# Prompt attention scores on two row halves of TensorE, sampled value products in one shape, sampled blocks in twos, seven cache buffers

## The chip, the cores and the metric

The kernel runs on one core of one Trainium2 chip. The metric is the device time of one execution in microseconds (us); lower is better. The core has TensorE (PE in the profile; its loads of the stationary operand are listed as PEld), VectorE (DVE), ScalarE (ACT), GpSimd (POOL) and SyncE (SP), whose queue issues most of the DMAs. TensorE multiplies a stationary operand, held in an array of 128 rows (contraction) by 128 columns (output partitions), by a moving operand that streams through it.

## The reference

One step of a streaming encoder with two layers: a convolution layer, then an attention layer, each followed by a SwiGLU feed-forward block. Two groups go through it together: 512 prompt frames of one new stream, and 16 frames of each of 8 running streams (the samples). Only the attention is touched. There are 16 heads of 64 features. The prompt attends to its own keys, in chunks of 64 frames, with a learned bias by distance; a sample attends to 512 cached keys and its own 16 new ones:

```
def band_attention_sample(q, k_all, v_all, table):
    s = jnp.einsum("bqhd,bkhd->bhqk", q, k_all) * scale + bias
    p = jax.nn.softmax(s, axis=-1)
    return jnp.einsum("bhqk,bkhd->bqhd", p, v_all)
# prompt, for each chunk of 64 queries: the same over the 576 keys that end with the chunk,
# keys ahead of the stream's start masked with -1e30
```

All is 32-bit floating point.

## The kernel before

All activations are kept with features on the partitions: `h` is 128 x 8 x 640, the first 128 of the 640 columns being the samples and the other 512 the prompt. Weight products that need full precision split both operands into a high part (`fp32r`, a rounded type of 32 bits) and the low rest and add three products, high x high, low x high, high x low (`mm3`, L196 to L202). The program runs the convolution layer, the first feed-forward block, the attention stage (about 694 to 1002 us of the profiled execution) and the second feed-forward block.

*The attention stage* works through 8 pairs of heads (the loop at L1418). For each pair `proj_kq` projects keys and queries of the pair into `kt` and `qt`, 128 x 640, where rows 0 to 63 are the first head and 64 to 127 the second. `proj_v` projects values for two pairs at once, `proj_o` and `halves` the output. The order of a pair's own steps is written out by hand in the strings `BO` (pairs 0 to 6) and `BL` (the last pair) at L67 and L68; each token is a letter for the step and a digit for its instance:

- `a` (`head_a`, L1259): the prompt scores of one head, its row maxima and its softmax. A head has 64 features, half of the array's rows, so the kernel fills the other half with low parts: `QQ` holds the query's high part in the head's own rows and its low part in the other rows; `KK` holds the key's high part in both halves, `KL` the key's low part in both. Then two matmuls per query tile on all 128 rows (L1285, L1286) give all products. The four query tiles need 512, 384, 128 and 256 key columns, in this order (`ORD`). Making `KK`, `KL` and `QQ` takes two ScalarE copies (L1271, L1272), one GpSimd copy (L1273) and three VectorE subtractions (L1275 twice, L1277), all on 64 rows x 512. Scores go to PSUM: three tiles to `wide`, the fourth to a part of `st`, both from the two large buffers of `w2t()`. `addmax` (L1193) adds the bias and takes the row maximum on VectorE, `softmax_rows` takes exponentials on ScalarE.
- `s` (`samp_a`, L1331): the scores of four streams, for both heads of the pair: loads four cache tiles, two of keys and two of values, from a pool of `CB = 8` buffers (L1337, on SP's queue); then matmuls with 32 stationary columns for each stream, so that four streams fill the four column strips of the array (form 128\*32; L1342 for cached keys, L1345 for new ones), into `st` of the head before; then bias, maximum, exponentials.
- `b` (`head_b`): transposes the prompt's probabilities; `t` and `n` (`samp_b` and its `rest`): transpose the sampled ones, `t` for the 512 cached keys, `n` for the 64 new ones (L1364).
- `p` (`pair_c`, L1318): the prompt's value product, each head on 64 of the array's columns (form 128\*64).
- `c` (`samp_c`, L1371): the sampled value product, four streams on four column strips, in five steps: four over cached values on 128 rows (L1378, form 128\*32) and one over the new values on the 64 rows of this block (L1382, form 64\*32).
- `d`: scales, transposes and splits the sampled output (L1386 to L1397).
- `o`, `q` in `BL`: one or two steps of an output projection (`halves`), placed there as filler.

Transposes, value products and the `d` steps share the two PSUM buffers of `amt()`; projections use the two of `mmt()`. The strings give the order of priority. Each engine's final order is fixed when the program is built: TensorE's queue takes matmuls of a projection where the next step of the pair would have to wait. `qt` has one buffer and `kt` two.

Of the kernel before, what the change touches and what calls it, by code (L numbers as in the profile page):

```python
# [15 lines left out]
P = 128  # L16
# [42 lines left out]
CB, QB, KB = 8, 1, 1  # L59
# [7 lines left out]
BO = "a0 s0 a1 s1 b0 b1 t0 n0 p0 c0 d0 t1 n1 c1 d1"  # L67
BL = "a0 o2 s0 a1 o2 s1 q2 t0 q2 n0 b0 q2 b1 q2 c0 q2 d0 t1 q2 n1 o2 c1 o2 d1 p0 o2"  # L68
# [14 lines left out]
def tile_trunk(ctx, tc, xT, vecs, hist, w_pw1, w_pw2, w_in0, w_out0, w_os0, w_in1, w_out1, w_os1,  # L83
# [1052 lines left out]
    nc.gpsimd.memset(BP[:, :, 0:256], 0.0)  # L1136
    BS = ap.tile([P, 576], F32, name="BS", tag="BS")
# [121 lines left out]
    def head_a(p, hh):  # L1259
        kt, qt = kts[p], qts[p]  # L1260
        r = slice(hh * DH, hh * DH + DH)
        S = sp.tile([P, 1280], F32, tag="S", name=nm("S"))
        mx = ap.tile([P, 4], F32, tag="mx", name=nm("mx"), bufs=3)
        sm = ap.tile([P, 4], F32, tag="sm", name=nm("sm"), bufs=3)
        wide = w2t()
        st = w2t()
        ro = slice(DH - hh * DH, 2 * DH - hh * DH)
        KK = ap.tile([P, 512], F32R, tag="KK", name=nm("KK"), bufs=KB)
        KL = ap.tile([P, 512], F32R, tag="KL", name=nm("KL"), bufs=KB)
        QQ = ap.tile([P, 512], F32R, tag="QQ", name=nm("QQ"), bufs=KB)  # L1270
        nc.scalar.activation(out=KK[r], in_=kt[r, P:], func=AF.Copy)  # L1271
        nc.scalar.activation(out=QQ[r], in_=qt[r, P:], func=AF.Copy)  # L1272
        nc.gpsimd.tensor_copy(KK[ro], KK[r].bitcast(F32))  # L1273
        for to in (r, ro):
            nc.vector.tensor_tensor(out=KL[to], in0=kt[r, P:], in1=KK[r].bitcast(F32),  # L1275
                                    op=ALU.subtract)
        nc.vector.tensor_tensor(out=QQ[ro], in0=qt[r, P:], in1=QQ[r].bitcast(F32),  # L1277
                                op=ALU.subtract)
        pss = []
        for i in ORD:  # L1280
            n = (i + 1) * P
            o = SOFF[i]
            q = slice(i * P, (i + 1) * P)
            ps = st[:, 640:896] if i == 1 else wide[:, o:o + n]
            nc.tensor.matmul(ps, QQ[:, q], KK[:, 0:n], start=True, stop=False)  # L1285
            step_end[0] = nc.tensor.matmul(ps, QQ[:, q], KL[:, 0:n], start=False, stop=True).ins  # L1286
            pss.append(ps)
        for ii, i in enumerate(ORD):
            n = (i + 1) * P
            o = SOFF[i]  # L1290
            addmax(S[:, o:o + n], pss[ii], BP[:, hh, 512 - n:512], mx[:, ii:ii + 1])
        rs = softmax_rows(S, mx, sm, [(SOFF[i], (i + 1) * P) for i in ORD])
        for ii, i in enumerate(ORD):
            n = (i + 1) * P
            o = SOFF[i]
            nc.vector.tensor_scalar(out=S[:, o:o + n], in0=S[:, o:o + n],
                                    scalar1=rs[:, ii:ii + 1], scalar2=None, op0=ALU.mult)
        return S, st
# [32 lines left out]
    def samp_a(p, u, st):  # L1331
# [18 lines left out]
        addmax(S, st[:, 0:576], BS, mx[:, 0:1])  # L1350
# [3 lines left out]
    def samp_b(u, S):  # L1354
        v0 = 64 * u
        tr = amt()
        for k in range(4):
            step_end[0] = nc.tensor.transpose(tr[:, k * P:(k + 1) * P],
                                              S[:, k * P:(k + 1) * P], ident).ins
        PT = ap.tile([P, 640], F32, tag="PTs", name=nm("PTs"), bufs=1)  # L1360

        def rest():
            tn = amt()
            step_end[0] = nc.tensor.transpose(tn[0:v0 + 64, 0:P], S[:, 512 - v0:576], ident).ins  # L1364
            nc.vector.tensor_copy(PT[v0:v0 + 64, 512:640], tn[v0:v0 + 64, 0:P])
            return PT

        nc.scalar.activation(out=PT[:, 0:512], in_=tr, func=AF.Copy)
        return rest

    def samp_c(p, u, PT, rs, VC):  # L1371
        v0 = 64 * u
        VT = vts[p // 2]
        pv = amt()
        for k in range(5):
            for b in range(4):
                if k < 4:
                    nc.tensor.matmul(pv[32 * b:32 * b + 32, 0:P],  # L1378
                                     PT[:, k * P + 32 * b:k * P + 32 * b + 32],
                                     VC[b // 2][:, b % 2, k * P:(k + 1) * P], start=(k == 0), stop=False)  # L1380
                else:
                    step_end[0] = nc.tensor.matmul(  # L1382
                        pv[32 * b:32 * b + 32, 0:P],
                        PT[v0:v0 + 64, 512 + 32 * b:512 + 32 * b + 32],
                        VT[v0:v0 + 64, 0, (p % 2) * P:(p % 2) * P + P], start=False, stop=True).ins
        os_ = ap.tile([P, P], F32, tag="os", name=nm("os"), bufs=1)  # L1386
# [31 lines left out]
    for p in range(NP):  # L1418
# [8 lines left out]
        for op in (BL if p == NP - 1 else BO).split():  # L1427
            i = int(op[1])
            if op[0] == "a":
                ha[i] = head_a(p, i)  # L1430
            elif op[0] == "s":
                sa[i] = samp_a(p, i, ha[i][1])
            elif op[0] == "b":
                pt[i] = head_b(ha[i][0])
# [4 lines left out]
            elif op[0] == "c":  # L1439
                ps[i] = samp_c(p, i, ps[i], *sa[i][1:])  # L1440
# [247 lines left out]
```

## Time and profile before

| | |
|---|---|
| three runs | 1458.16, 1460.51, 1463.31 us; median 1460.51 |
| span of the profiled execution | 1460.0 us, 28194 instructions |
| TensorE busy | 1434.0 us (98%) |
| VectorE, ScalarE, GpSimd busy | 1138.9, 757.8, 297.6 us |
| granted TensorE clock | 0.999 of full speed |
| DMA over the span | 192.56 MB, 132 GB/s |

The time of the profiled execution outside its span is not given; the span lies within the three runs. A row of a group names the line, the engine, the operation, output<-inputs, for TensorE the array's shape in use (rows\*columns), the moving operand, and a count; then the busy time in us, the mean of one in ns, and the idle time ahead of it with what ended it. A row of the timeline begins with start and length in us; instructions of one line that follow each other are merged into one row, with their count. Matmuls overlap in the array, so the step from one start to the next says more than the length. Operations on 4-byte data that are not `fp32r` run as two passes, each with a row of its own.

### The profile page before, as it was taken

The numbers are of one execution on the slowest core, as the hardware profiler recorded it, in microseconds if no ns is written. First come the engines' busy times: TensorE is split into PE (matmuls) and PEld (weight loads), VectorE is DVE, ScalarE is ACT, GpSimd is POOL, SyncE is SP. The second block draws the span as 40 slices with busy tenths as digits, with TensorE's granted clock in tenths as the row PEclk, the third lists the DMA queues.
The fourth block names the chain that finished last, engine by engine and source line by source line (L and its number), as shares of the span: only waits on it lengthen the run. The fifth ranks groups of instructions, "written<-read, shape, count | busy, mean of one in ns | idle before, by whom it ended". The sixth has DMA issues, their size and how long they took to land. (4 is left out here: it accounts for less than half of the span.)

```text
span 1460.0 us, 28194 instructions
## 1 busy us (share of the span) xinstructions
PE 1434.0 (98%) x11022; PEld 1369.6 (94%) x11022; DVE 1138.9 (78%) x2520; ACT 757.8 (52%) x1628; POOL 297.6 (20%) x349
## 2 busy tenths in 40 slices
PE   9999999999999999999999999999999999999998
PEld 8998799999999999999987898878999999999998
DVE  6789867988888888756768668577898888888765
ACT  4666554654554554545654355443554564455453
POOL 5699120010111111013222121011011111111101
PEclk9999999999999999999999999999999999999999
DMA  7267434045444534425556554452125444444522
GB/s 243 73 180 187 126 86 146 14 135 150 131 108 118 163 92 135 116 88 193 181 163 213 173 192 162 138 200 67 44 82 143 135 113 129 137 120 109 155 66 72
DMA packets 66932, 192.56 MB, mean 132 GB/s; under 512 B 12144, under 2 KB 30320, under 8 KB 58480
## 3 DMA queue, kind: packets, MB, share of 16 engines
q1 hardware_dynamic: 52432, 160.58, 33.8%
q0 software_dynamic: 13504, 29.37, 9.9%
q8 instruction: 86, 1.41, 0.4%
q10 hardware_dynamic: 864, 0.83, 0.2%
q14 instruction: 46, 0.38, 0.1%
HBM read 179.14 MB, written 11.61 MB: 131 GB/s over the span
## 5 line engine op out<-in xcount | busy, mean ns | idle before, releaser
L439 PE MATMUL mm<-XH,whi 128*128 128x320 f32 x896 | 275.9, 310 | 2.9 <-ACT t L451 2.6
L439 PE MATMUL mm<-XH,wlo 128*128 128x320 f32 x896 | 276.1, 309 | 0.0
L439 PE MATMUL mm<-XL,whi 128*128 128x320 f32 x896 | 274.5, 309 | 0.0
L371 ACT ACTIVATE whi<-raw 128x512 fp32r<-128x512 f32 (+2 forms) x280 | 168.4, 613 | 135.2 <-PE mm L439 103.6
L199 PE MATMUL mm<-xh,whi 128*128 128x320 f32 (+2 forms) x640 | 200.2, 314 | 0.8 <-DVE h L702 0.4
L200 PE MATMUL mm<-xh,wlo 128*128 128x320 f32 (+2 forms) x640 | 198.2, 311 | 0.0
L372 DVE TENSOR_TENSOR wlo<-raw,whi 128x512 fp32r<-128x512 f32 (+2 forms) x280 | 183.9, 666 | 15.9 <-ACT whi L371 14.8
L201 PE MATMUL mm<-xl,whi 128*128 128x320 f32 (+2 forms) x640 | 195.9, 311 | 0.4 <-DVE xl L189 0.4
L439 PE MATMUL mm<-hid,whi 128*128 128x320 f32 x732 | 172.5, 311 | 5.5 <-DVE hid L372 3.1
L439 PEld LDWEIGHTS mm<-XH,whi 128*128 128x128 f32 x896 | 167.7, 188 | 4.9 <-ACT t L451 4.2
L439 PEld LDWEIGHTS mm<-XH,wlo 128*128 128x128 f32 x896 | 168.2, 188 | 0.0
L439 PEld LDWEIGHTS mm<-XL,whi 128*128 128x128 f32 x896 | 167.7, 188 | 0.0
L439 PEld LDWEIGHTS mm<-hid,whi 128*128 128x128 f32 x732 | 125.0, 188 | 8.8 <-DVE hid L372 4.2
L199 PEld LDWEIGHTS mm<-xh,whi 128*128 128x128 f32 x640 | 120.5, 188 | 4.0 <-ACT xh L187 1.5
L201 PEld LDWEIGHTS mm<-xl,whi 128*128 128x128 f32 x640 | 119.7, 188 | 1.2 <-DVE xl L189 0.8
L200 PEld LDWEIGHTS mm<-xh,wlo 128*128 128x128 f32 x640 | 120.5, 189 | 0.2
L439 PE MATMUL mm<-hid,wlo 128*128 128x320 f32 x366 | 113.0, 309 | 0.0
L439 PE MATMUL mm<-XH,slo 128*128 128x320 f32 x344 | 106.0, 308 | 0.0
L439 PE MATMUL mm<-XH,shi 128*128 128x320 f32 x344 | 105.8, 309 | 0.0
L439 PE MATMUL mm<-XL,shi 128*128 128x320 f32 x344 | 105.6, 308 | 0.0
L417 POOL DMA_DIRECT2D s<-in_w_in x38 | 22.1, 581 | 388.7 <-DVE wlo L372 151.8
L841 POOL TENSOR_TENSOR ca<-ca,cvt 128x512 f32<-128x512 f32 x60 | 91.9, 1532 | 17.8 <-ACT cvt L838 11.2
(275 smaller groups left out, 3370.8 us busy)
## 6 DMA issues: line engine op xcount, KB each, us to landing
raw<-in_w_in SPq DMA_DIRECT2D x38, 1024.0 KB
s<-in_w_in POOLq DMA_DIRECT2D x76, 256.0 KB, 4.2
raw<-in_w_os SPq DMA_DIRECT2D x24, 768.0 KB
cache<-in_ck SPq DMA_DIRECT2D x32, 512.0 KB
cache<-in_cv SPq DMA_DIRECT2D x32, 512.0 KB
raw<-in_w_pw SPq DMA_DIRECT2D x11, 1024.0 KB
s<-in_w_os POOLq DMA_DIRECT2D x48, 192.0 KB, 3.6
raw<-in_w_kq SPq DMA_DIRECT2D x8, 1024.0 KB
```

Of the source, the lines that this page charges most:

```text
L199: nc.tensor.matmul(ps, wh, xh, start=(first and i == 0), stop=False)
L200: nc.tensor.matmul(ps, wl, xh, start=False, stop=False)
L201: end = nc.tensor.matmul(ps, wh, xl, start=False, stop=(stop and i == last))
L371: put_end[1] = nc.scalar.activation(out=hi, in_=src, func=AF.Copy).ins
L372: put_end[0] = nc.vector.tensor_tensor(out=lo, in0=src, in1=hi.bitcast(F32), op=sub).ins
L417: nc.gpsimd.dma_start(s1, src[:, 2 * n:3 * n])
L439: last = nc.tensor.matmul(pt, wt, v, start=(first and k == i == 0), stop=(k == n - 1 and i == 2), skip_group_check=True)
L841: nc.gpsimd.tensor_tensor(out=acc, in0=acc, in1=pr, op=ALU.add)
```

## The change

1. `head_a` gives up its score matmuls. A new `heads_split` makes the scores of both heads at once, when token `a0` is reached: the high and low parts are made for both heads together on 128 rows x 512 (two ScalarE copies, two VectorE subtractions a pair, no GpSimd copy), and each head's three products run on its own 64 rows, the two heads alternating. Three query tiles of each head go to a large buffer of its own; the fourth goes to a buffer of `amt()`.
2. `samp_a` takes its own large buffer (`w2t()`) in place of `st`.
3. The fifth step of `samp_c` uses 128 rows: the transposed probabilities of the new keys (`pn`) are padded with zeros in the rows of the other block, from `Sn` (zeros in columns 576 to 639) or in `PN` (zeros in rows 0 to 63), both set once. The scaled output `os_` now lies in the block's own probability tile.
4. `BO` and `BL` put `a0 a1`, `s0 s1`, `t0 n0 t1 n1` (in `BO`) and `c0 c1`, `d0 d1` together; in `BO` the pair product `p0` comes ahead of `c0`, as before, now with `c1` behind `c0`.
5. `CB` is 7: seven cache buffers for the eight cache tiles of a pair. `Ss` has one buffer (and `Sn`), `PTs` two.

```
-CB, QB, KB = 8, 1, 1
+CB, QB = 7, 1
-BO = "a0 s0 a1 s1 b0 b1 t0 n0 p0 c0 d0 t1 n1 c1 d1"
-BL = "a0 o2 s0 a1 o2 s1 q2 t0 q2 n0 b0 q2 b1 q2 c0 q2 d0 t1 q2 n1 o2 c1 o2 d1 p0 o2"
+BO = "a0 a1 s0 s1 b0 b1 t0 n0 t1 n1 p0 c0 c1 d0 d1"
+BL = "a0 o2 a1 o2 s0 s1 q2 t0 q2 n0 b0 q2 t1 q2 b1 n1 q2 c0 c1 q2 d0 o2 d1 o2 p0 o2"
...
+    Sn = ap.tile([P, 640], F32, name="Sn", tag="Sn")
+    nc.gpsimd.memset(Sn[:, 576:640], 0.0)
+    PN = ap.tile([P, P], F32, name="PN", tag="PN")
+    nc.gpsimd.memset(PN[0:64, :], 0.0)
...
+    def heads_split(p):
+        kt, qt = kts[p], qts[p]
+        KH, KL, QH, QL = (ap.tile([P, 512], F32R, tag=t, name=nm(t)) for t in ("KH", "KL", "QH", "QL"))
+        for src, hi, lo in ((kt, KH, KL), (qt, QH, QL)):
+            nc.scalar.activation(out=hi, in_=src[:, P:], func=AF.Copy)
+            nc.vector.tensor_tensor(out=lo, in0=src[:, P:], in1=hi.bitcast(F32), op=ALU.subtract)
+        wide = [w2t(), w2t()]
+        narrow = [amt(), amt()]
+        pss = [[], []]
         for i in ORD:
             n = (i + 1) * P
             o = SOFF[i]
             q = slice(i * P, (i + 1) * P)
-            ps = st[:, 640:896] if i == 1 else wide[:, o:o + n]
-            nc.tensor.matmul(ps, QQ[:, q], KK[:, 0:n], start=True, stop=False)
-            step_end[0] = nc.tensor.matmul(ps, QQ[:, q], KL[:, 0:n], start=False, stop=True).ins
-            pss.append(ps)
+            for hh in range(2):
+                pss[hh].append(narrow[hh][:, 0:n] if i == 1 else wide[hh][:, o:o + n])
+            for j, (a, b) in enumerate(((QH, KH), (QL, KH), (QH, KL))):
+                for hh in range(2):
+                    r = slice(hh * DH, hh * DH + DH)
+                    step_end[0] = nc.tensor.matmul(pss[hh][-1], a[r, q], b[r, 0:n], start=j == 0,
+                                                   stop=j == 2).ins
+        return pss
...
-        S = ap.tile([P, 576], F32, tag="Ss", name=nm("Ss"), bufs=2)
+        S = ap.tile([P, 576], F32, tag="Ss", name=nm("Ss"), bufs=1) if u else Sn
...
-        PT = ap.tile([P, 640], F32, tag="PTs", name=nm("PTs"), bufs=1)
+        PT = ap.tile([P, 512], F32, tag="PTs", name=nm("PTs"), bufs=2)
...
-            step_end[0] = nc.tensor.transpose(tn[0:v0 + 64, 0:P], S[:, 512 - v0:576], ident).ins
-            nc.vector.tensor_copy(PT[v0:v0 + 64, 512:640], tn[v0:v0 + 64, 0:P])
-            return PT
+            step_end[0] = nc.tensor.transpose(tn[:, 0:P], S[:, 512 - v0:640 - v0], ident).ins
+            pn = PN if u else ap.tile([P, P], F32, tag="PM", name=nm("PM"), bufs=1)
+            nc.vector.tensor_copy(pn[v0:, :], tn[v0:, 0:P])
+            return PT, pn
...
-                        PT[v0:v0 + 64, 512 + 32 * b:512 + 32 * b + 32],
-                        VT[v0:v0 + 64, 0, (p % 2) * P:(p % 2) * P + P], start=False, stop=True).ins
-        os_ = ap.tile([P, P], F32, tag="os", name=nm("os"), bufs=1)
+                c = slice(k * P + 32 * b, k * P + 32 * b + 32)
+                step_end[0] = nc.tensor.matmul(
+                    pv[32 * b:32 * b + 32, 0:P], PT[:, c] if k < 4 else pn[:, 32 * b:32 * b + 32],
+                    VC[b // 2][:, b % 2, k * P:(k + 1) * P] if k < 4
+                    else VT[:, 0, (p % 2) * P:(p % 2) * P + P], start=k == 0, stop=k == 4).ins
+        os_ = S[:, 0:P]
...
-                sa[i] = samp_a(p, i, ha[i][1])
+                sa[i] = samp_a(p, i, w2t())
```

More of the change, by code (lines that the diff above doesn't have):

```diff
@@ L1257, in tile_trunk @@
     ORD = (3, 2, 0, 1)
-    def head_a(p, hh):
+    def heads_split(p):
         kt, qt = kts[p], qts[p]
[L1261 to L1279, printed above, removed]
+        KH, KL, QH, QL = (ap.tile([P, 512], F32R, tag=t, name=nm(t)) for t in ("KH", "KL", "QH", "QL"))
[5 more added lines that the diff above has]
+        pss = [[], []]
         for i in ORD:
@@ L1283, in head_a @@
             q = slice(i * P, (i + 1) * P)
-            ps = st[:, 640:896] if i == 1 else wide[:, o:o + n]
-            nc.tensor.matmul(ps, QQ[:, q], KK[:, 0:n], start=True, stop=False)
-            step_end[0] = nc.tensor.matmul(ps, QQ[:, q], KL[:, 0:n], start=False, stop=True).ins
-            pss.append(ps)
+            for hh in range(2):
[6 more added lines that the diff above has]
+        return pss
+    def head_a(p, hh, pss):
+        S = sp.tile([P, 1280], F32, tag="S", name=nm("S"))
+        mx = ap.tile([P, 4], F32, tag="mx", name=nm("mx"), bufs=3)
+        sm = ap.tile([P, 4], F32, tag="sm", name=nm("sm"), bufs=3)
         for ii, i in enumerate(ORD):
@@ L1429, in tile_trunk @@
             if op[0] == "a":
-                ha[i] = head_a(p, i)
+                if i == 0:
+                    pss = heads_split(p)
+                ha[i] = head_a(p, i, pss[i])
             elif op[0] == "s":
-                sa[i] = samp_a(p, i, ha[i][1])
+                sa[i] = samp_a(p, i, w2t())
             elif op[0] == "b":
-                pt[i] = head_b(ha[i][0])
+                pt[i] = head_b(ha[i])
             elif op[0] == "t":
```

18 lines of the change are left out of this document (6 added, 12 removed).

## The prediction

> **What bounds the kernel now.** I read the page's totals first, then the TensorE timeline of the attention stage (694 to 1002 us, the only stretch whose code changes), then the busy times of that stretch and its groups by form.
>
> ```profile
> span 1460.0 us, 28194 instructions
> PE 1434.0 (98%) x11022; PEld 1369.6 (94%) x11022; DVE 1138.9 (78%) x2520; ACT 757.8 (52%) x1628; POOL 297.6 (20%) x349
> ```
>
> ```profile
> 694.00:1002.00 308.00, 303.25 (x2743) 263.54 (x2743) 213.50 (x639) 151.50 (x407) 55.79 (x93) 1.00 0.51 169
> 965.00:1002.00 37.00, 34.18 (x361) 25.71 (x361) 26.67 (x78) 15.15 (x39) 1.24 (x2) 1.00 0.26 93
> ```
>
> The rows of the second view give length, then busy PE, PEld, DVE, ACT and POOL, clock, DMA share and GB/s. TensorE is busy 303.25 of 308 us at the full clock (1.00) and idle 4.75 us, of which 2.82 fall in the last 37 us, where no projection is left to fill with. So the stage ends when TensorE has worked off its queue. Busy time says nothing about how densely it works; for that I read start to start, because the matmuls overlap.
>
> ```profile
> 694.83 0.39 PE L1285 MATMUL w<-KK,QQ 128*128 128x512 f32 x1
> 695.06 0.40 PE L1286 MATMUL w<-KL,QQ 128*128 128x512 f32 x1
> 695.29 0.34 PE L1285 MATMUL w<-KK,QQ 128*128 128x384 f32 x1
> 695.48 0.34 PE L1286 MATMUL w<-KL,QQ 128*128 128x384 f32 x1
> 695.65 0.22 PE L1285 MATMUL w<-KK,QQ 128*128 128x128 f32 x1
> 695.71 0.28 PE L1286 MATMUL w<-KL,QQ 128*128 128x128 f32 x1
> 695.82 0.33 PE L1285 MATMUL w<-KK,QQ 128*128 128x256 f32 x1
> 695.99 0.28 PE L1286 MATMUL w<-KL,QQ 128*128 128x256 f32 x1
> 696.11 0.28 PE L199 MATMUL mm<-whi,xh 128*128 128x256 f32 x1
> ...
> 699.94 0.28 PE L201 MATMUL mm<-xl,whi 128*128 128x256 f32 x1
> 700.06 0.28 PE L199 MATMUL mm<-xh,whi 128*128 128x256 f32 x1
> 700.27 1.07 PE L1342 MATMUL w<-cache,qbd 128*32 128x512 f32 x8
> 701.16 0.29 PE L1345 MATMUL w<-kt,qbd 128*32 128x64 f32 x8
> 701.38 0.39 PE L200 MATMUL mm<-xh,wlo 128*128 128x256 f32 x1
> 701.60 0.28 PE L201 MATMUL mm<-xl,whi 128*128 128x256 f32 x1
> 701.72 0.28 PE L199 MATMUL mm<-xh,whi 128*128 128x256 f32 x1
> ```
>
> Two things are seen. One head's scores take 696.11 - 694.83 = 1.28 us; the slots are 0.23 us at 512 columns, 0.19 and 0.17 (mean 0.18) at 384, 0.06 and 0.11 at 128, 0.17 and 0.12 at 256. And leaving the full 128x128 shape costs time. The last full matmul before the sampled block has a slot of 0.21 where its neighbour of the same form has 0.12: 0.09 us to go in. After it the first full matmul has 0.22 for 0.12: 0.10. What the last tiled matmul loses is hidden in a merged row; I estimate it as the way in, 0.09. One trip out of the full shape and back is then 0.28 us.
>
> **The change part by part.** *Scores.* Removed are 16 matmuls a pair (8 a head), 2 x 1.28 = 2.56 us. Added are 24 on 64 rows each, in twelve twos: three products of four widths, each for both heads. The trace has no two matmuls on different row halves, so the price lies between one slot for a two and two slots. The nearest rows are the column tiles:
>
> ```profile
> 710.97 0.61 PE L1342 MATMUL w<-cache,qbd 128*32 128x512 f32 x4
> 711.40 0.29 PE L1345 MATMUL w<-kt,qbd 128*32 128x64 f32 x8
> L1342 PEld LDWEIGHTS w<-cache,qbd 128*32 128x32 f32 x128 | 2.8, 108 | 3.2 <-issue 1.9 <-DVE S L1296 0.2
> ```
>
> Four matmuls of 512 columns on four column tiles leave together, 0.43 us for all four. Their loads overlap as well: 128 loads of 108 ns would be 13.8 us one after another and cover 2.8. I take one slot for a two, since disjoint tiles of the array run at once here. A round is 0.23 + 0.18 + 0.11 (the slower of the two at 128 columns) + 0.12 = 0.64 us, three rounds 1.92, and one trip 0.28: 2.20 us a pair. Saved: 0.36 us, over eight pairs **2.9 us**. With two slots for each two it is 3.84 + 0.28 = 4.12, a loss of 1.56 a pair, 12.5 us in all.
>
> The Trainium skill, page TensorE: Matmul & The Clock Gate, section Measured speedup vs the span model, gives 3.07 times for four row tiles at once, not 4; if twos reached the same 77%, a round would be an estimated 0.83 us and the whole sum 1457 us, where the 0.43 us for four column tiles gives 1453; no run here shows row tiles.
>
> *Sampled value products in one shape.*
>
> ```profile
> 730.26 1.08 PE L1378 MATMUL am<-cache,PTs 128*32 128x128 f32 x32
> 731.27 0.42 PE L1382 MATMUL am<-vt,PTs 64*32 64x128 f32 x8
> 731.63 0.50 PE L1285 MATMUL w<-KK,QQ 128*128 128x512 f32 x1
> ```
>
> Four steps over cached keys take 1.01 us, the fifth, on 64 rows, 0.36. A step is two passes of four tiles of 128 columns; from the 0.43 us above for 512 columns a pass is 0.11 and a step 0.22. So the first four have 1.01 - 0.88 = 0.13 us too much, the price of changing from 128x32 to 64x32 inside the block. With 128 rows in all five that goes: 16 blocks x 0.13 = **2.1 us**. Rows cost nothing, columns are unchanged.
>
> *Blocks in twos.* There are 16 sampled score blocks, 16 value blocks and 8 pair products. Read from the first at 700.27 to the last,
>
> ```profile
> 1000.34 2.37 PE L1326 MATMUL am<-PT,vt 128*64 128x512 f32 x16
> ```
>
> the TensorE timeline makes 33 trips of these 40 blocks (some already touch). If s0 with s1, and p0 with c0 and c1, stay together, 16 trips are left: 17 x 0.28 = 4.8 us saved. If projections are put between s0 and s1 and between c0 and c1, as now between blocks, about 33 remain and nothing is saved. s0 needs the wide buffer of head 0, s1 that of head 1, and the row maxima that release them are read one after the other:
>
> ```profile
> 696.14 0.69 DVE L1194 CUSTOM_DVE_ANT_0 S<-w,BP 128x512 f32<-128x512 f32 x1 [0.82 <-PE w L1286]
> ...
> 697.79 0.08 DVE L1194 DVE_READ_ACCUMULATOR2_ANT mx<- 128x1 f32 x1
> ```
>
> A head's four take 697.87 - 696.14 = 1.73 us; s0 itself takes 1.1 (700.27 to 701.38). So s1 may be 0.6 us from ready when s0 ends, and a filler may come between. I take half, **2.4 us**, ends 0 and 4.8. If the narrow tiles are late (they now come from the two buffers that d0 and d1 transpose into), a score block falls in two: another 0.28 a pair, 2.2 us, kept for the upper end.
>
> *Other engines.*
>
> ```profile
> L1275 DVE TENSOR_TENSOR KL<-kt,KK 64x512 fp32r<-64x512 f32 x30 | 22.3, 743 | 4.2 <-ACT KK L1271 3.8
> L1277 DVE TENSOR_TENSOR QQ<-qt,QQ 64x512 fp32r<-64x512 f32 x16 | 11.0, 685 | 1.1 <-ACT QQ L1272 0.9
> L189 DVE TENSOR_TENSOR olo<-am,ohi 128x512 fp32r<-128x512 f32 x7 | 4.8, 689 | 9.5 <-ACT ohi L187 9.5
> L1271 ACT ACTIVATE KK<-kt 64x512 fp32r<-64x512 f32 x15 | 9.4, 630 | 16.8 <-PE w L1285 10.4 <-DVE kt L1211 6.3
> L187 ACT ACTIVATE ohi<-am 128x512 fp32r<-128x512 f32 x7 | 4.2, 595 | 17.3 <-PE am L1326 17.3
> ```
>
> VectorE drops 32 x 0.743 + 16 x 0.685 = 34.7 us and adds 16 x 0.689 = 11.0; ScalarE drops 32 x 0.63 = 20.2 and adds 16 x 0.595 = 9.5; GpSimd loses its 16 copies. All of it lies beside the projections on TensorE, so I take nothing; the most it can give is the 4.75 us of TensorE idle time. The wider transposes of the new keys keep their 128 moving columns, the two memsets come once: nothing.
>
> *Waits added.* The sampled score block now waits for row maxima (above); behind it in TensorE's queue stand projections, and its own row maximum and exponentials wait for it. With seven cache buffers each cache tile takes the buffer of the tile one place later in the pair before (the eighth that of the first in its own pair). So the second key tile of s0 needs a buffer that c0 of the pair before frees, the second of s1 one that c1 frees; today each takes that of its own kind.
>
> ```profile
> SPq L1337 <- PE am L1378: 39.6, 12, 9.0
> SPq L1337 <- PE w L1345: 33.8, 14, 8.5
> ```
>
> ```profile
> cache<-in_ck SPq DMA_DIRECT2D x32, 512.0 KB
> ```
>
> SP already waits there (us in total, times, longest), for 0.52 MB a tile, and behind a waiting load stand the bias rows, the weight loads and the key output, on which GpSimd's bias and ScalarE's weight split wait. From c0 to the second key tile of s1 five tiles of 0.52 MB must land. At 169 GB/s for a share of 0.51, the stage row above, all engines would move 331 GB/s: 7.9 us at best, 15.5 at the stage's rate. The cover is the projection of the following pair. I take nothing, with an end of 2 us a pair.
>
> *Sum*, against the profiled execution's 1460.0 us (the median of the three runs is 1460.5, so what lies around the span is lost in their scatter): 1460.0 - 2.9 - 2.1 - 2.4 = 1452.6, **1453 us**.
>
> **The rivals.**
> *Loads of the two halves go one after another.* Then a two costs no less than twice the 0.11 us slot at 128 columns: three rounds of 0.23 + 3 x 0.22 are 2.67, with the trip 2.95 a pair, 0.39 more than now, 3.1 in all. With 2.1 and 2.4 saved: 1460.0 + 3.1 - 4.5 = **1459 us**. Against it: the overlapping loads of the column tiles. For it:
>
> ```profile
> L1382 PEld LDWEIGHTS am<-vt,PTs 64*32 64x32 f32 x128 | 2.5, 104 | 3.2 <-issue 3.0 <-DVE h L1255 0.2
> ```
>
> A load on 64 rows lasts 104 ns, on 128 rows 108 (above), so halving the rows doesn't shorten it, and 24 loads stand where 16 stood. The Trainium skill, page TensorE: Matmul & The Clock Gate, section LDWEIGHTS (loading the stationary operand), says the same, that a load lasts by its columns and not its rows; by that rule this rival's 1459 us holds unless the halves load at once, which no run here shows.
> *The blocks don't stay together* (the change doesn't do what it says): some 33 trips remain and the score blocks are cut in two: 1460.0 - 2.9 - 2.1 + 2.2 = **1457 us**. For it: today's order puts fillers wherever a buffer is late.
> *Cache loads become the wait (slower).* If s0 and s1 run before the five tiles have landed and the projections are used up, TensorE stands. In the trace c0 starts at 730.26, with the next pair's scores directly behind (731.63); a sampled block some 6 us after c0 would stand 2 us (7.9 against 5.9). Seven pairs: 14 us, 1460.0 - 7.4 + 14 = **1467 us**. It decides as soon as the gap from c0 to s1 is under some 8 us.
> *The row halves don't run at once (slower).* 1460.0 + 12.5 - 4.5 = **1468 us**. No row here shows such a two; it decides if the second of a two starts a whole slot after the first.
>
> **How the numbers follow.** The forecast has 0.52, the blocks that don't stay together 0.15, serial loads 0.10, cache loads 0.13, serial halves 0.10. The forecast's own range is 1445 (2.9 + 2.1 + 4.8 + 4.75 saved) to 1455 (nothing from the twos). Over the cases the range is **1445 to 1467**, which leaves out the serial halves and the longer cache waits. A measurement tells 0.3% from no change, 4.4 us: faster is under 1456.1, slower over 1464.9. Faster gets 0.49 of the forecast, 0.06 of the second case and 0.02 of the others: **0.57**. Slower gets 0.08 of the cache loads, 0.09 of the serial halves and 0.02 else: **0.19**. The rest, **0.24**, is the same.
>
> **What would show it.** Right: the twelve twos of a score block start two at a time, a 512-column two has a slot near 0.23 us, a block with its trip lasts about 2.2 us; value blocks are 40 rows of one form with about 1.25 us; 16 trips besides; TensorE idle stays below 5 us in the stage. Wrong: slots of 0.45 in twos (serial halves), 0.22 at 128 columns (serial loads), TensorE idle ahead of the L1342 products with cache loads landing late, or idle ahead of them by the row maxima.

## The result and the profile after

The changed kernel takes 1475.06 us (median of six runs, 1472.04 to 1478.93); the kernel before, run beside it, 1460.84. The ratio is 1.0103, 95% interval 1.0093 to 1.0113: 14 to 15 us slower. The forecast was 1453, its range ended at 1467. In five of the variants below (b_cb7, a_cb8, a_old, a_kv, a_hold_kres) one run was far slower, 2336 to 6021 us; their medians leave it out, and in a_kv and a_old, where it was the profiled run, no times are read from its rows.

The totals of the page of after, then the stage's busy times in after and, over the same length, in before (length, then busy PE, PEld, DVE, ACT and POOL, clock, DMA share, GB/s):

```profile
span 1474.1 us, 28218 instructions
...
PE 1440.5 (98%) x11086; PEld 1370.6 (93%) x11086; DVE 1118.9 (76%) x2488; ACT 746.7 (51%) x1612; POOL 280.5 (19%) x335
```

```profile
690.00:1014.00 324.00, 311.73 (x2825) 265.69 (x2824) 192.87 (x612) 142.31 (x397) 43.26 (x81) 1.00 0.49 164
```

```profile
690.00:1014.00 324.00, 319.25 (x2859) 279.23 (x2858) 227.17 (x673) 163.56 (x434) 58.14 (x96) 1.00 0.50 166
```

VectorE and ScalarE lost work as planned, and TensorE is idle 12.3 us of 324 where it was idle 4.75. That is half of the loss. The other half is seen in start-to-start steps of TensorE's matmuls, added up by kind and with idle time taken out, from the stage's first projection to the start of the matmul behind the last product of `p0` (us, rows rounded; the "kept keys" kernel is a_kres below). A trip is one leaving of the full array shape for a score, value or pair block. (Eight transposes of before, L1364 in form 128\*64, aren't counted: between projections of 256 columns their steps are those of the eight in form 128\*128, 0.12 us ahead of them, 0.03 to the next start, then 0.20.)

| | before | after | change | kept keys |
|---|---|---|---|---|
| prompt scores | 21.2 | 22.2 | +1.0 | 22.2 |
| sampled scores | 19.2 | 23.8 | +4.6 | 18.0 |
| sampled value products | 22.5 | 19.0 | -3.5 | 19.1 |
| pair products | 18.4 | 18.4 | 0 | 18.4 |
| projections | 201.5 | 203.6 | +2.1 | 202.7 |
| transposes | 25.9 | 27.4 | +1.5 | 27.1 |
| idle | 4.7 | 12.3 | +7.5 | 5.5 |
| sum | 313.6 | 326.7 | +13.1 | 313.0 |
| trips | 33 | 54 | +21 | 48 |

The way into a trip falls on the matmul ahead of it, often a projection: at the 0.09 us of the prediction, 21 more trips are an estimated 1.9 us, about the projections' +2.1.

*Idle.* TensorE's waits in this stretch of after, by engine, line and releaser (us in total, times, longest), and then the two largest waits of SP's queue at the cache loads:

```profile
PE w L1343 <- DMA cache<-in_ck: 6.9, 5, 2.0
PE mm L199 <- DVE h L1259: 1.4, 3, 0.8
```

```profile
SPq L1338 <- PE am L1381: 58.3, 14, 9.6
...
SPq L1338 <- PE w L1343: 23.2, 11, 10.9
```

The sampled scores wait for key tiles (with 1.1 us of another kind, 8.0 us of idle time stand ahead of them), and the loads of cache tiles wait for the value products (L1381) to free a buffer: 58.3 us, where before the row was 39.6. One place shows the chain, in TensorE's timeline and in that of SP's queue, where each block loads two key tiles and then two value tiles:

```profile
773.10 1.08 PE L1381 MATMUL am<-cache,PTs 128*32 128x128 f32 x32
774.00 0.40 PE L1381 MATMUL am<-vt,PM 128*32 128x128 f32 x8
774.21 1.03 PE L1343 MATMUL w<-cache,qbd 128*32 128x512 f32 x4
...
776.20 1.08 PE L1381 MATMUL am<-cache,PTs 128*32 128x128 f32 x32
777.09 0.40 PE L1381 MATMUL am<-vt,PN 128*32 128x128 f32 x8
...
780.15 0.62 PE L1343 MATMUL w<-cache,qbd 128*32 128x512 f32 x2 [2.04 <-DMA cache<-in_ck]
```

```profile
766.15 0.38 SPq L1338 DMA_DIRECT2D cache<-in_ck  x1
...
774.21 0.33 SPq L1338 DMA_DIRECT2D cache<-in_ck  x1
774.62 1.31 SPq L1338 DMA_DIRECT2D cache<-in_cv  x2
777.30 1.11 SPq L1338 DMA_DIRECT2D cache<-in_ck  x2
```

```profile
774.00:782.00 8.00, 5.96 (x89) 3.88 (x81) 1.50 (x5) 0.44 (x2) 0.00 (x0) 1.00 0.92 308
```

The loads at 766.15 and 774.21 are the two key tiles of one block, an `s1`, and the two rows of L1343 are its two halves. The first half runs at 774.21, right behind `c0` of the pair before. The second tile gets the buffer that this `c0` frees: its load starts at 774.21, and the products on it start at 780.15, 5.9 us later, the last 2.04 us of them idle. Both value blocks stand 3.1 us apart, so four more tiles (two of values and, as `c1` ends at 777.30, the next pair's two key tiles) are sent for within 3.6 us of this load. The last row gives 308 GB/s at a share of 0.92 for these 8 us, near the 331 that the prediction took for all engines (a_hold reaches 393 at 0.99, in the last section). The other waits for key tiles read alike: 6.0 us from load to products behind the next `c0` (814.58 to 820.57), 4.9 in a third place (898.95 to 903.88, a buffer that `s0` frees), and 5.7 and 6.7 in the last turn (981.30 to 986.95, 982.49 to 989.19).

Before, the same two value blocks stood 10.3 us apart (starts at 768.13 and 778.41), and `s1` comes in the main behind the second of them:

```profile
769.24 0.80 SPq L1337 DMA_DIRECT2D cache<-in_ck  x2
```

The two key tiles are sent for at the end of `c0`, as in after, but the products on the second start at 780.61, some 11 us after its load. In the seven turns of before from one pair to the next this cover is never under 10.9 us; in after it is 4.9 to 7.6 us in five of them.

*Sampled scores in halves.* The row at 774.21 is half a block: two streams of the first key tile, alone on two of the four column strips, 0.96 us to the next matmul, where four streams take 0.86 in a whole block (734.53 - 733.67 in a_kres below). The starts of L1343 show six of the sixteen blocks cut in two by key tile (before two, with kept keys none). So a cut block costs about twice, and four more are an estimated 3.4 to 3.8 of the +4.6 us.

*Prompt scores in pieces.* TensorE's timeline of after, a score block's main part, and a block's narrow tile a few us away from its own:

```profile
726.29 0.50 PE L1281 MATMUL w<-KH,QL 64*128 64x512 f32 x2
726.62 0.39 PE L1281 MATMUL w<-KL,QH 64*128 64x512 f32 x2
726.85 0.34 PE L1281 MATMUL w<-KH,QH 64*128 64x384 f32 x2
727.03 0.34 PE L1281 MATMUL w<-KH,QL 64*128 64x384 f32 x2
727.21 0.34 PE L1281 MATMUL w<-KL,QH 64*128 64x384 f32 x2
727.38 0.22 PE L1281 MATMUL w<-KH,QH 64*128 64x128 f32 x2
727.44 0.27 PE L1281 MATMUL w<-KH,QL 64*128 64x128 f32 x2
727.55 0.28 PE L1281 MATMUL w<-KL,QH 64*128 64x128 f32 x2
...
742.05 0.38 PE L1281 MATMUL am<-KH,QH 64*128 64x256 f32 x1
742.27 0.28 PE L1281 MATMUL am<-KH,QL 64*128 64x256 f32 x1
742.38 0.28 PE L1281 MATMUL am<-KL,QH 64*128 64x256 f32 x1
742.59 0.30 PE L1346 MATMUL w<-kt,qbd 128*32 128x64 f32 x4
```

Each row with x2 holds both heads, in the trace 2 to 5 ns apart: the halves do run at once, in slots of 0.23, 0.18 and 0.06 to 0.11, as taken. But in four of the eight blocks the 256-column tile runs for one head by itself (here 0.54 us for three products, the other head's three elsewhere). By the code its two PSUM buffers are those of `amt()`, which the value products and transposes use too; that they come free one at a time is a reading of this order, no row shows it. The eight blocks lie in 27 pieces.

### The profile page after: what moved, and what is told of

The parts are those of the page before. It is cut to its first block, busy times and chain, and to the rows that moved or that the text cites. A ratio compares the mean times of both kernels' runs of the same rounds, so it can differ in the third digit from the quotient of the medians.

```text
span 1474.1 us, 28218 instructions
## 1 busy us (share of the span) xinstructions
PE 1440.5 (98%) x11086; PEld 1370.6 (93%) x11086; DVE 1118.9 (76%) x2488; ACT 746.7 (51%) x1612; POOL 280.5 (19%) x335
```

## The experiments

The theory after the result: the loss is made of waits for key tiles, which the new order with seven buffers holds up (theory W in the expectations), on top of blocks that fall into pieces. Rivals: seven buffers cost by themselves; the pieces, with their trips, are all of it (theory T); the new order costs in itself, whatever the buffers (theory O); a part of the change costs that the profile doesn't show as a wait. Each ratio is to the kernel before, run on the same chip; TensorE's queue is ordered anew for each kernel, so differences between variants hold the effect of that order too. Some variants also run stretches of the stage at half the TensorE clock (last section); before, after and a_kres have none there.

### Seven buffers alone

**b_cb7**: the kernel before with one number changed.

```
-CB, QB, KB = 8, 1, 1
+CB, QB, KB = 7, 1, 1
```

> The kernel before with seven cache buffers in place of eight, nothing else. Theory W (cache loads are the new wait): the second key tile of a block now waits for the value block of the pair before also in the old order, so TensorE idles ahead of L1342 and the time rises by 4 to 12 us, to 1465 to 1473 us. Theory T (what costs is that TensorE leaves its full shape more often, 54 times in place of 33): the buffers matter little, 1459 to 1463 us.

Measured 1459.47 us, ratio 1.0001 (0.999 to 1.0013). The waits of SP's queue there:

```profile
SPq L1337 <- PE am L1378: 43.6, 12, 9.0
```

Four us more of waiting for value products (39.6 before), and none of it reaches TensorE. Seven buffers cost nothing in the old order.

### Buffers in the new order

**a_pt1** and **a_cb8**: after with one `PTs` buffer in place of two (that makes room), then also eight cache buffers (the change of `CB` is in a_cb8 alone).

```
-PT = ap.tile([P, 512], F32, tag="PTs", name=nm("PTs"), bufs=2)
+PT = ap.tile([P, 512], F32, tag="PTs", name=nm("PTs"), bufs=1)
...
-CB, QB = 7, 1
+CB, QB = 8, 1
```

> A control: the changed kernel with one buffer instead of two for the transposed sampled probabilities (PTs), which sets free the 2 KB a partition that an eighth cache buffer needs. Both theories: within 3 us of the changed kernel, 1472 to 1478 us; the two value blocks of a pair come further apart, which by theory T may cost up to 2 us.

> The control with eight cache buffers. Theory W: the 6.9 us in which L1343 waits for cache loads go, and part of the idle time of the last pair, so 6 to 11 us under the control, about 1466 us. Theory T: at most 2 us under the control, 1473 us.

1502.7 us, ratio 1.0301 (1.0283 to 1.032), and 1493.16, 1.0222 (1.0201 to 1.0243). The one buffer costs 28 us over after (69 trips, 19.1 us idle), where within 3 us were expected: a bad control. Inside it the eighth cache buffer gives 5 us by the two profiled runs and some 10 by the medians.

**a_lows_cb8**: after with eight buffers, room made by keeping `KL` and `QL` in one of the prompt's probability buffers.

```
-CB, QB = 7, 1
+CB, QB = 8, 1
...
+lows = sp.tile([P, 1280], F32, tag="S", name=nm("lows")).bitcast(F32R)
+KL, QL = lows[:, 0:512], lows[:, 512:1024]
```

> The kernel after with an eighth cache buffer and nothing else of its order, its blocks or its other buffers changed; the room comes from keeping the low parts KL and QL in one of the prompt's probability buffers. Loads waiting for a buffer: the idle time ahead of the sampled scores (8.0 us after) falls to some 3 us, fewer sampled score blocks are cut in two by key tile, and the kernel is 5 to 10 us faster than after, 1465 to 1470. Rival, the loads are late because of the transfer rate and not of the buffers: no change, 1474 to 1477. Rival, the shared probability buffer holds up the scores: slower than after, over 1478, with idle time ahead of the scores.

1471.74 us, 1.0085 (1.0072 to 1.0099). The idle time ahead of the sampled scores falls from 8.0 to 1.5 us and sampled scores from 23.8 to 20.0, but only 3 us come back where 5 to 10 were expected, with an interval that overlaps that of after: prompt scores rise to 24.8 in 58 trips, other waits are 2.7 us longer, and one stretch at half clock costs up to 1.7. The queue's order differs too: from the load of `s1`'s second key tile to its products there are 7.6 us or more in every turn, so the run doesn't tell the buffer from the places.

**a_kv** and **a_kv_look** (the same kernel): keys in four buffers, values in three of their own.

> The changed kernel with its seven cache buffers split into four for key tiles and three for value tiles: each key tile takes the buffer of the same tile of the pair before, and the last value tile of a pair waits for that pair's first value block. 61 trips by the queue's order (54). Theory W (key tiles wait for value products): the 8.0 us idle ahead of the sampled scores fall under 2, their 23.8 us go back to about 19; 7 more trips cost 2 us and the second value block may wait up to 2 us in some pairs: 1464 to 1469 us. Theory O (the new order itself makes the waits): idle time and time within 3 us of the changed kernel, 1473 to 1479 us.

> One look at a_kv. Theory W: no idle time ahead of the sampled scores by key loads, but 3 to 8 us ahead of value products by value loads. Theory O: as much idle time ahead of the sampled scores as in the changed kernel.

1478.1 us, 1.0125 (1.011 to 1.0141), where theory W had expected 1464 to 1469. The waits of TensorE in a_kv_look, 1477.16:

```profile
PE am L1381 <- DMA cache<-in_cv: 3.7, 3, 2.8
```

There sampled scores fall to 19.2 us and the idle time ahead of them to 1.3, as expected, but the wait has moved from keys to values, value products rise from 19.0 to 22.3, and trips to 61; seven buffers in another split are no cure.

**a_kres** (kept keys): the key tiles of the first block are kept and used by all sixteen, which leaves out 30 key loads; values have four buffers.

```
+if tag == "ck" and len(keys) == 2:
+    cache.append(keys[i])
+    continue
...
+if tag == "ck":
+    keys.append(t)
```

> The changed kernel with the cached keys loaded once: the two key tiles of the first block are used by all 16 blocks (the other 30 key loads are left out, so the sampled attention uses the wrong keys), values in four buffers of their own. No sampled score block can wait for a load, no load for a block of another kind. 48 trips by the queue's order (54). Theory W (key loads held up by value products are the cause): the 8.0 us idle ahead of the sampled scores and most of their 4.6 us more go, 9 to 13 us under the changed kernel, 1462 to 1466 us. Theory O (the order itself): only the 6 trips fewer, 1.6 us, 1471 to 1475 us.

1461.38 us, 1.0009 (1.0 to 1.0019): 13.7 less than after, all but about 1 us of its loss. Its column stands in the table: idle 5.5, sampled scores 18.0. The same turn from one pair to the next, in TensorE's timeline:

```profile
732.56 1.08 PE L1388 MATMUL am<-cache,PTs 128*32 128x128 f32 x32
733.46 0.40 PE L1388 MATMUL am<-vt,PM 128*32 128x128 f32 x8
733.67 1.04 PE L1350 MATMUL w<-cache,qbd 128*32 128x512 f32 x8
734.53 0.29 PE L1353 MATMUL w<-kt,qbd 128*32 128x64 f32 x8
734.64 1.04 PE L1350 MATMUL w<-cache,qbd 128*32 128x512 f32 x8
```

Both score blocks follow `c0` whole, with nothing between. What is left is that the order, rid of its waits, only equals before: 48 trips and prompt scores of 22.2 us keep the forecast's gain from coming. (This kernel also moves 15.7 MB less, 30 x 0.52, and its queue has 6 trips fewer, an estimated 1.6 us; so it takes the waits for buffers, the traffic and some pieces away together.)

### Prompt scores in one piece

**a_whole**: `ORD = (1, 3, 2, 0)`, the narrow tile first. It was also to hold the block back until the low parts are there, but the hold was tied to a VectorE instruction, and the blocks lie in 33 pieces, more than before it; so what is measured is in the main the tile order.

> The changed kernel (seven buffers) with the score block held in one piece: the narrow tile comes first in the order of the query tiles, so that the block begins only when its last buffers are free, and no matmul of it is queued ahead of the last low part. Theory T: the 27 pieces of score blocks become some 8 to 12, some 15 trips of 0.28 us and the solo products of one head go, 4 to 6 us under the changed kernel, about 1470 us. Theory W: within 2 us of the changed kernel, the waits for cache loads stay at some 7 us.

1465.79 us, 1.0049 (1.0034 to 1.0064); 59 trips, prompt scores 24.0, idle 7.2, sampled scores 17.8. The blocks are less whole than in after, yet 9 us come back, though three stretches at half clock cost up to 5.1. From the load of `s1`'s second key tile to its products there are now 8.0 us or more in every turn, and no sampled score waits. That agrees with waits and speaks against pieces as the whole cause.

**a_hold**: the products with low parts first, the second head first, and every matmul of the block tied behind the first.

```
-    ORD = (3, 2, 0, 1)
+    ORD = (1, 3, 2, 0)
...
-            for j, (a, b) in enumerate(((QH, KH), (QL, KH), (QH, KL))):
-                for hh in range(2):
+            for j, (a, b) in enumerate(((QL, KH), (QH, KL), (QH, KH))):
+                for hh in (1, 0):
...
+                    with tc.issue_after(first) if first else nullcontext():
```

> The changed kernel (seven buffers, same order of tokens) with the score block held in one piece by the order alone: the product that needs the last low part and the last narrow buffer comes first, and the other 23 matmuls of the block are queued behind it. In the queue's order the score blocks then are 12 pieces instead of 27 and TensorE leaves its full shape 37 times instead of 54. Theory T: 17 trips of 0.28 us and some 2 us of one head's products running alone go, about 6.5 us under the changed kernel, 1468 us, with the waits for cache loads left. Theory W: the trips cost little, within 2 us of the changed kernel unless the waits of L1343 for cache loads change too, in which case the time follows TensorE's idle time.

1469.61 us, 1.0075 (1.006 to 1.009): 37 trips, prompt scores 19.5, but 13.5 us idle. The blocks lie in 12 pieces for 27, and TensorE now waits at other places, the largest of them:

```profile
PE mm L199 <- ACT ohi L187: 3.1, 1, 3.1
PE am L1361 <- ACT Sn L1191: 1.8, 1, 1.8
PE w L1345 <- issue: 1.6, 1, 1.6
```

**a_hold_kres**: a_hold with the kept keys of a_kres.

> The kernel a_hold (score block in one piece) with the cached keys loaded once, as in a_kres: 37 trips, no wait for key loads. What it shows is the best that the change's order can give without the cache wait. By the sum (1460.0 + 1 us of four more trips - 1.7 to 2.6 us of scores - 2.6 us of value products): 1456 us if TensorE's idle time falls back to that of the kernel before, 4.7 us; 1462 to 1465 us if the idle time of the held block, which waits for its last buffer, stays near 10 us as in a_hold_cb8.

1470.39 us, 1.0064 (1.0044 to 1.0084), no better than a_hold: a miss. Idle is 13.9 us, 7.1 of it ahead of transposes and 4.6 ahead of projections, and as in a_hold half clock costs up to 5.1 us more. In a_hold 7.7 us or more lie between the load of `s1`'s second key tile and its products, so its key loads were in time already, and other waits had taken their place.

**a_hold_cb8** (a_hold with the eight buffers of a_lows_cb8) and **a_mix_cb8** (the same, the last pair not tied):

> The kernel a_hold with eight cache buffers; the place for the eighth comes from keeping the low parts of keys and queries in a buffer of the prompt's probabilities (S). 39 trips by the queue's order. Theory W: what is left of the waits for cache loads goes, 5 to 8 us under a_hold, about 1460 us or less. Theory T: within 2 us of a_hold, since seven buffers cost nothing in the old order.

> The kernel a_hold_cb8 with the last pair's score block let loose again (its matmuls may start as soon as each is ready), since at the last pair no projection is left to fill the wait for the block's last buffer. Theory: 2 to 5 us of TensorE idle time and its clock drop around the last pair go, at a cost of 2 to 3 trips: 1460 to 1463 us, at best level with the kernel before.

1464.73 us, 1.0039 (1.0024 to 1.0054), with prompt scores 18.6, sampled scores 17.4 and idle 10.0: the best version of the new order with all its loads, still slower than before. And 1469.64, 1.0066 (1.0051 to 1.0081): freeing the last pair loses 4 to 5 us, 1.8 of it idle time and up to 3.4 a longer stretch at half clock (13.65 us from 981.48 on, for 6.83 in a_hold_cb8). Over a_hold, a_hold_cb8 has 3.5 us less idle time (the 3.1 us behind `ohi` are gone) and one 3.4 us stretch at half clock less, together the size of its 4.9 us. Since a_hold_kres shows key loads not to bind a_hold, why the eighth buffer, or the order that comes with it, eases these waits stays open.

**a_hold_serial**: a_hold, one head's three products ahead of the other's, so that twos are given up.

```
...
+            for hh in (1, 0):
+                for j, (a, b) in enumerate(((QL, KH), (QH, KL), (QH, KH))):
```

> The kernel a_hold with the two heads' products one head after the other inside a query tile, in place of by turns; same matmuls, same buffers, 39 trips for 37. If the row halves run at once only when they alternate, as the trace of the changed kernel reads: some 0.6 us a round less overlap, 8 x 1.9 = 12 to 15 us over a_hold, about 1483 us. If the halves don't run at once anyway: within 2 us of a_hold.

1475.0 us, 1.0107 (1.009 to 1.0123): 5.4 us over a_hold, where 12 to 15 were expected; prompt scores are 21.4 for 19.5. But the built queue still alternates heads in many places: 58 of its 192 score products start within 40 ns of the one before, in a_hold 48, in after 75. So the run does not tell what halves one after the other would cost.

### One shape, twos, and the price of a trip

**b_one**: before with part 3 of the change alone (128 rows in all five steps, `PTs` in one buffer).

> The kernel before with the sampled value products in one shape alone (Sn, PN and PM padded with zeros, everything else as before). Both theories: 16 changes of shape inside a block go, 0.13 us each, 2 us under the kernel before, 1458 us; if the single Ss buffer delays a block, no gain.

1457.45 us, 0.9986 (0.9976 to 0.9996), 2 us less than before. The first value block in its timeline:

```profile
728.18 1.08 PE L1384 MATMUL am<-cache,PTs 128*32 128x128 f32 x32
729.08 0.40 PE L1384 MATMUL am<-vt,PM 128*32 128x128 f32 x8
729.41 0.50 PE L1289 MATMUL w<-KK,QQ 128*128 128x512 f32 x1
```

729.41 - 728.18 = 1.23 us where before had 731.63 - 730.26 = 1.37: 0.14 a block, 2.2 in all. This is the version that beats both kernels.

**b_twos**: b_one with the transposes and value products of both sampled blocks put together in `BO`, two `PTs` buffers, eight cache buffers; the sampled scores stay apart.

```
-BO = "a0 s0 a1 s1 b0 b1 t0 n0 p0 c0 d0 t1 n1 c1 d1"
+BO = "a0 s0 a1 s1 b0 b1 t0 n0 t1 n1 p0 c0 c1 d0 d1"
```

> The kernel b_one (old scores on all 128 rows, eight cache buffers, value products in one shape) with the value blocks of a pair side by side (BO with t0 n0 t1 n1 p0 c0 c1 d0 d1, two PTs buffers); the sampled score blocks and the last pair stay as before. If twos of value blocks save a trip each in most of seven pairs, 1 to 2 us under b_one, 1455 to 1457 us; if the new places of t1, n1 and d0 cut other blocks in pieces (the full-row score blocks cost nothing when cut), the trips come back and the time is that of the kernel before or more, 1458 to 1463 us.

1462.74 us, 1.0015 (1.0006 to 1.0024): 4 us slower than b_one (0.0029 of 1460). 34 trips against 33, and 8.3 us idle against 4.9. The twos of value blocks save no trip and cost waiting, without the row halves and with eight buffers; none of this waiting is for a cache load.

**a_old**: after in the old `BO` and `BL`, one `PTs` buffer, so beside a_pt1.

> The changed kernel with the token order of the kernel before (and one PTs buffer, as there), seven cache buffers: only the scores on two row halves and the value products in one shape are left of the change. 68 trips by the queue's order, in place of 54 (changed) and 33 (before). Theory T: 14 trips more than the changed kernel, 4 us, less what the cache waits lose since seven buffers cost nothing in this order: 1470 to 1479 us, well over the kernel before. Theory W: the waits for cache loads go with the order, and the time falls to 1455 to 1463 us.

1483.68 us, 1.0168 (1.0151 to 1.0185), 19 us less than a_pt1: with one buffer the old order is far the better. But it is 24 us over before, and both theories missed it (W 1455 to 1463, T 1470 to 1479). This order loses nothing by seven buffers (b_cb7) nor by part 3 (b_one), so what is left is the row halves with their new places in PSUM (parts 1 and 2), or how these meet the fewer buffers; the new order isn't to blame here. Its 68 trips (by the queue's order), 35 more than before, are an estimated 9 to 10 us at 0.26 to 0.29 each; what the rest is stays open.

**b_trips** and **b_full**: before with 32 small products in the projections of keys and queries, on 64 rows (a trip each) or on 128 (none). They write columns that the next product overwrites.

```
+nc.tensor.matmul(pt[:, 504:512], ident[0:64, :], ident[0:64, 0:8], start=True, stop=True)
```

> The kernel before with one extra small product on 64 rows (8 columns, into a part of the projection's PSUM buffer that nobody reads) ahead of each of the 32 accumulation groups of the key and query projections: 32 more trips out of the full shape and nothing else. Theory T: 32 x 0.28 us = 9 us over the kernel b_full, about 1470 us. If a trip costs TensorE nothing it can't hide: the same as b_full.

> The control of b_trips: the same 32 small products on all 128 rows, so no trip. Both theories: 32 x 0.06 to 0.1 us, 2 to 3 us over the kernel before, about 1462 us.

1476.14 us, 1.0112 (1.0097 to 1.0127), and 1467.94, 1.0053 (1.0038 to 1.0068): (1476.14 - 1467.94) / 32 = 0.256 us a trip. One of them in the two timelines, b_trips ahead:

```profile
698.33 0.28 PE L201 MATMUL mm<-wlo,xh 128*128 128x256 f32 x1
698.54 0.39 PE L1208 MATMUL mm<-ident 64*128 64x8 f32 x2
698.86 0.39 PE L199 MATMUL mm<-xh,whi 128*128 128x256 f32 x1
699.08 0.28 PE L200 MATMUL mm<-xh,wlo 128*128 128x256 f32 x1
```

```profile
698.69 0.28 PE L201 MATMUL mm<-wlo,xh 128*128 128x256 f32 x1
698.81 0.28 PE L1208 MATMUL mm<-ident 128*128 128x8 f32 x2
698.95 0.36 PE L199 MATMUL mm<-xh,whi 128*128 128x256 f32 x1
699.15 0.28 PE L200 MATMUL mm<-xh,wlo 128*128 128x256 f32 x1
```

699.08 - 698.33 = 0.75 against 699.15 - 698.69 = 0.46: 0.29 by the rows. b_full itself lies 7.7 us over before, where 2 to 3 were expected (last section). The Trainium skill, TensorEngine Tiling (Array Packing), section Key Properties, says that a change of the tiling mode drains TensorE; the rows agree for the row halves and give it a size, while the 64-column transposes of before (first section) show no such cost.

## Why the prediction was wrong, point by point

*The row halves* ("one slot for a two"): held. Slots of 0.23, 0.18 and 0.06 to 0.11 us on after's timeline; neither serial halves (0.45) nor serial loads (0.22 at 128 columns) appear in these blocks. The lower speed-up of row tiles that the prediction drew from the Trainium skill is not seen in these twos.

*The price of a trip*, 0.28: held, 0.256 to 0.29. *One shape*, 2.1: held, 2 us in b_one.

*The scores' saving*, 2.9: not got. The step took each block as whole, one trip a pair. The kernel makes 27 pieces of eight blocks, and prompt scores rise by 1.0 us in place of falling. The prediction kept "another 0.28 a pair" for late narrow tiles; the narrow tile in fact also loses its partner on the other half. In 12 pieces (a_hold, a_hold_cb8) prompt scores do fall, by 1.7 and 2.6 us: the price of the products was right, the block in one piece was not.

*Blocks in twos*, 2.4 with ends 0 and 4.8: failed on the sign. With one trip for each of the eight score blocks the forecast's 16 to 33 are 24 to 41 in all; the kernel makes 54. b_twos shows the part of the value blocks by itself: no trip saved, 4 us lost. Zero was no lower bound: a wait in a block lets other work cut in, and steps moved together bring their loads, buffers and successors together too.

*Waits added*, "I take nothing, with an end of 2 us a pair", covered by "the projection of the following pair": this is the step that decided. The cover was too short: 8.0 us of idle time ahead of the sampled scores and 4.6 us more in sampled scores, most of it in halved blocks, make up 12.6 of the 13.1 us. The rival of the cache loads had the place (idle ahead of L1342, now L1343), the occasion (`c0` frees a buffer too shortly before `s1`) and nearly the price, 14 us. It had the tile wrong: not the fifth tile after `c0` is waited for, 7.9 us at best, but the first, `s1`'s second key tile, which in two of the turns gets a buffer of `c0` where the prediction gave it one of `c1`, and whose products start 4.9 to 6.7 us after its load; and TensorE waits in four turns, not in seven. What the prediction missed is that the rival's condition, a gap from `c0` to `s1` under 8 us, was to be had from the strings: the cover had been the distance between `c0` and `c1`, some 10 us here, and the change takes that distance away. a_kres takes the loads away and gets nearly all of the loss back. In the prediction's terms the other gains and losses about cancel: value products give 3.5 us, more than the 2.1 forecast, and trips and pieces take them back.

*The rivals as alternatives*: they were weighed one at a time, and two came together. With the pieces' 1457 us and 14 us of cache waits on top, the sum is 1471, close to the 1475 measured. The range reached neither the pair nor its scatter.

*Other engines at nothing*: held in after (besides the 8.0 us, TensorE is idle 4.3 us there, before 4.75), but not in the tied variants, where ScalarE's `ohi` costs 3.1 us at one place.

Open: why parts 1 and 2 cost as much as they do in the old order (a_old), what the eighth buffer does for a_hold, and how much of a_kres is the buffers, how much the traffic and how much the order. An eighth buffer with the strings of after cleared the waits and gave back 3 us, since the queue's order differs as well.

## What to carry to other kernels

When steps of two blocks are moved together, follow each buffer that they free to the load that it holds up, and measure the time from that release to the load's first user: the distance between the old places may have been the cover. Count a saved change of array shape only if nothing in the block can wait; one late operand splits it, and then the change is paid twice and concurrent halves lose their partners. Rivals with a common cause are added up, not weighed against each other.

## What the runs showed of the hardware

*The clock after idle time.* Four stretches of 3.4 us in a_hold, by the view of busy times:

```profile
785.00:788.40 3.40, 0.26 (x2) 0.20 (x2) 3.25 (x14) 2.83 (x12) 0.00 (x0) 1.00 0.99 393
788.40:791.80 3.40, 3.40 (x19) 3.17 (x20) 0.02 (x1) 0.00 (x0) 0.00 (x0) 0.50 1.02 363
791.80:795.20 3.40, 1.77 (x23) 1.22 (x23) 2.80 (x13) 1.15 (x2) 0.00 (x0) 1.00 0.04 14
795.20:798.60 3.40, 3.40 (x33) 1.62 (x23) 3.37 (x14) 0.78 (x3) 0.71 (x1) 0.50 0.58 131
```

After a stretch with TensorE busy 0.26 of 3.40 us the granted clock is 0.50 for the next; after one busy 1.77 of 3.40 too. A stretch at half clock costs up to 1.7 us, so that a wait is paid once more; the stages of before, after and a_kres have none, a_hold and a_hold_kres three such stretches, a_hold_cb8 two. Busy time alone doesn't decide it: from 993.20 to 996.60 a_hold is busy 1.60 of 3.40 us, and the next 3.40 us run at 1.00. The Trainium skill, TensorE: Matmul & The Clock Gate, section What's actually happening, has the half clock after an idle window of about 3.4 us; here the window was only half idle the second time.

*Small products are dear.* Each of b_full's 32 products of 8 columns in the full shape costs 7.7 / 32 = 0.24 us (1467.94 - 1460.27), two passes and the late start of the next matmul (0.20 for 0.12); by the rows 0.46 - 2 x 0.12 = 0.22.
